# GpSimd instead of VectorE for the weight scales and for the inverse roots of queries and keys in a two-layer hybrid trunk

## The chip, the core and the metric

The kernel runs on one core of one Trainium2 chip. The metric is the device time of one execution in microseconds (us); the number that counts is the median of the runs.

## The reference

`x` is 512 tokens by 2048 columns. Two layers follow one another, each with one mixer of three parallel branches:

```python
h = rmsnorm(x, norm_g)                       # over 2048 columns
proj = h @ w_in                              # 2048 x 7696, float32
y_conv = B * (conv3(C * H) + bias) * silu(G)            # 4 x 512 columns
q, k = rmsnorm(sb_q, qn_g), rmsnorm(sb_k, kn_g)         # per head of 128
y_sb   = stick_breaking(q, k, sb_v) * silu(sb_g)        # 8 heads of 128
y_gla  = rmsnorm(gla(gl_q, gl_k, gl_v, decay(gl_lr))) * silu(gl_g)   # 4 heads
x = x + concat(y_conv, y_sb, y_gla) @ w_out  # 2048 x 2048
```

All weights are float32 in HBM and are read once per execution. What the change touches is not a step of the reference itself but two helpers: a power of two by which each block of weights is scaled before it is split into half-precision parts, and `rsqrt(mean(q*q) + eps)` of the query and key heads.

## The kernel before, in words

**Blocks of weights.** A layer's weights are cut into 38 blocks of 256 columns (one of 272): 30 of `w_in`, 8 of `w_out`; 76 in all, numbered along `specs`. A block is loaded by two DMAs of 1 MB (`fetch`, L341) into one of two staging tiles `st`. Then, for every block but the first:

1. `wmax` (L352): ScalarE squares both halves and adds them up per partition, two instructions of 128x2048, into `wm`.
2. `wscale`: GpSimd adds the sums up over the partitions (`partition_all_reduce`, L362, tile `wgm`). VectorE adds the two halves (L363, `wq`), masks the exponent (L371), and makes two powers of two by integer arithmetic on the bits: `ws` (L375), the scale, and `wp` (L377), from which `wu` (L379) follows, the factor that undoes the scale behind the matmul.
3. `whi` (L415): ScalarE writes `wh = half(st * ws)`. `wlo` (L421): VectorE writes `wl = half(st * ws - wh)`. One pair per half block; three tiles of each kind exist, so that the second half of a block waits until TensorE has read a half of the block before.
4. TensorE multiplies three times (high by high, high by low, low by high).

For 3 of the 8 blocks of `w_out` in layer 0 and 4 in layer 1 (`QUICK`) seven sums of sub-blocks take the place of eight products; ScalarE and VectorE split each of the seven (L450, L451) and VectorE makes the sums in place (L456 to L462). TensorE works them off at L698 with evictions at L709 to L727 between.

**Order.** `weights()` hands out block i, fetches block i + 2 and lets block i + 1 be scaled and split, at a raised priority; `issue_after` puts ScalarE's squares of a block behind the last `wh` of the block before it. Beyond that, and outside the first 40 us or so, which stand in an order written by hand for VectorE and ScalarE, a scheduler orders each engine's instructions when the program is built. Each engine works its own list off in order; an instruction that waits holds up those behind it.

**Stages of a layer**, with the times of layer 0 in the trace: GLA projections and the short convolution (to some 280 us), four rounds of stick-breaking attention (280 to 680), each of four blocks (V, gate, Q, K), the rest of the convolution (to 715), the eight blocks of `w_out` (to 870), whose last block is interleaved with the norm of the next layer.

**Query and key.** For each of the 16 Q and K blocks ScalarE copies the result out of PSUM (`raw`, L1198) and squares it (L1200), VectorE adds up over each head (`qs`, L1201) and makes eight inverse roots per partition: `qu` (L1203), `rsqrt_bits` (L207 to L214: a first guess from the bits, then three Newton steps of three instructions), a product with `wu` (L1206), all of 128x8. Then it scales `raw` (L1209 for Q, 64 instructions at L1214 for K), and ScalarE (L1218) and VectorE (L1219) split the result into `qp`, which is transposed by DMA.

Of the kernel before, what the change touches and what calls it, by code (L numbers as in the profile page):

```python
# [8 lines left out]
I32 = mybir.dt.int32  # L9
U8 = mybir.dt.uint8  # L10
AF = mybir.ActivationFunctionType
ALU = mybir.AluOpType
# [5 lines left out]
P = 128  # L18
EPS = 1e-6
# [20 lines left out]
def hybrid_trunk(ctx, tc, x, norm_g, w_in, conv_w, conv_b, sb_qn_g, sb_kn_g,  # L40
                 gla_w_up, gla_b_up, gla_on_g, w_out, out):
    nc = tc.nc
    V, S, G, T = nc.vector, nc.scalar, nc.gpsimd, nc.tensor
# [23 lines left out]
    def nm(s):  # L67
        uid[0] += 1
        return f"{s}_{uid[0]}"

    def sm(n, tag, bufs=None):
        return small.tile([P, n], F32, tag=tag, name=nm(tag), bufs=bufs)

    def wk(shape, tag, bufs=None, dt=F32):
        return work.tile(shape, dt, tag=tag, name=nm(tag), bufs=bufs)
# [4 lines left out]
    def bank(pool, tag):  # L80
        return pool.tile([P, 512], F32, tag=tag, name=nm("ps" + tag))
# [72 lines left out]
    r = 0  # L154
# [16 lines left out]
    def allmax(src, n, tag):  # L171

        gm = sm(n, tag + "gm")
        G.partition_all_reduce(gm, src, P, RED.absmax)
        return gm
# [28 lines left out]
    def rsqrt_bits(dst, src, scale, n, tag):  # L204

        m = sm(n, tag + "rm")
        V.tensor_scalar(m, src, scale, EPS, ALU.mult, ALU.add)  # L207
        r = sm(n, tag + "r0")
        V.tensor_scalar(r.bitcast(I32), m.bitcast(I32), -0.5, float(0x5F375A86), ALU.mult, ALU.add)
        t = sm(n, tag + "rt")  # L210
        for i in range(3):
            V.tensor_tensor(t, r, r, ALU.mult)
            V.scalar_tensor_tensor(t, t, -0.5, m, ALU.mult, ALU.mult)
            V.scalar_tensor_tensor(dst if i == 2 else r, t, 1.5, r, ALU.add, ALU.mult)  # L214

    identb = const.tile([P, P], BF16, tag="identb", name="identb")
    V.tensor_copy(identb, ident)
# [25 lines left out]
    xun = const.tile([P, depth], F32, tag="xun", name="xun")  # L243
# [73 lines left out]
    mixun = {}  # L317
# [37 lines left out]
    def wscale(i):  # L355

        l, src, cols = specs[i]

        m = sm(1, "wq")
        if i:  # L360
            gm = sm(2, "wgm")
            G.partition_all_reduce(gm, peak.pop(i), P, RED.add)  # L362
            V.tensor_scalar(m, gm[:, 0:1], gm[:, 1:2], 2.0 ** -120, ALU.add, ALU.max)  # L363
        else:

            ps = bank(psm, "m")[:, :1]
            pk = peak.pop(i)
            for j, (a, b) in enumerate(((ones, pk[:, 0:1]), (ones, pk[:, 1:2]), (pk[:, 2:3], pk[:, 2:3]))):
                T.matmul(ps, a.to_broadcast([P, P]), b, start=j == 0, stop=j == 2)
            V.tensor_scalar(m, ps, 2.0 ** -120, None, ALU.max)  # L370
        V.tensor_scalar(m.bitcast(I32), m.bitcast(I32), 0x7F000000, None, ALU.bitwise_and)  # L371

        lift = int(i in quick)
        sc = sm(1, "ws")
        V.tensor_scalar(sc.bitcast(I32), m.bitcast(I32), -0.5, float((204 - lift) << 23), ALU.mult, ALU.add)  # L375
        p2 = sm(1, "wp")
        V.tensor_scalar(p2.bitcast(I32), m.bitcast(I32), 0.5, float((50 + lift) << 23), ALU.mult, ALU.add)  # L377
        u = sm(1, "wu", bufs=6)
        V.tensor_tensor(u, p2, mixun[l] if src is w_out else xun[:, l:l + 1], ALU.mult)  # L379
        loaded[i] = ([], u)  # L380
        scales[i] = sc

# [179 lines left out]
    xhigh(0, 0, mix)  # L562
    xsquare(1)
    wscale(0)
    whi0(0, 0, S)
    whi0(0, 1, V)
# [40 lines left out]
    for l in range(depth):  # L607
# [3 lines left out]
        def project_cols():  # L611

            w, u = weights()
            ps = [bank(psp, "p") for _ in range(2)]
            for h in range(2):
                wh, wl = w[h]
                for c, o in enumerate(ps):
                    cs = slice(c * P, (c + 1) * P)
                    for kk in range(HK):
                        k = h * HK + kk  # L620
                        st_ = (h == 0 and kk == 0)
                        en = (h == 1 and kk == HK - 1)
                        T.matmul(o, wh[:, kk, cs], xh[:, :, k, :], start=st_, stop=False)  # L623
                        T.matmul(o, wh[:, kk, cs], xl[:, :, k, :], start=False, stop=False)  # L624
                        T.matmul(o, wl[:, kk, cs], xh[:, :, k, :], start=False, stop=en)  # L625
            return ps, u
# [153 lines left out]
        def mixscale(j, m, tag, top=11.0):  # L780

            pow2(pmix[:, j:j + 1], m, -top, tag)
            s_ = sm(1, tag + "smix")
            V.reciprocal(s_, pmix[:, j:j + 1])
            return s_
# [77 lines left out]
        for tag in ("qT", "kT"):  # L863
            ps, u = project_cols()
# [3 lines left out]
            gm = allmax(mx, 2, tag)  # L868
            m = sm(1, tag + "m")
            V.tensor_tensor(m, gm[:, 0:1], gm[:, 1:2], ALU.max)  # L870
            p2 = sm(1, tag + "p2")
# [15 lines left out]
        for p in range(2):  # L887
            ps, u = project_cols()
            gmx = sm(1, "ggm")
            gg.append(gate(ps, u, gmx))  # L890
            m = sm(1, "gb")
# [208 lines left out]
        def go():  # L1100
            if later:
                later.pop(0)()
# [64 lines left out]
        for j in range(4):  # L1167
            bm = sm(2, "bm")
            ps, u = project_toks(xh, xl)

            vhl = wk([P, 2, NT, GW], "v", dt=F16)
            vh, vl = vhl[:, 0], vhl[:, 1]
            for b in range(2):
                bs = slice(2 * b, 2 * b + 2)
                v3 = ps[b].rearrange("p (a c) -> p a c", a=2)
                S.activation(vh[:, bs, :], v3, AF.Copy, scale=2.0 ** -14)
                V.scalar_tensor_tensor(vl[:, bs, :], v3, 2.0 ** -14, vh[:, bs, :], ALU.mult, ALU.subtract)
            V.tensor_reduce(bm[:, 0:1], vh, AX.XY, ALU.max, apply_absolute_value=True)
            vu = sm(2, "vu")
            V.tensor_scalar(vu[:, 0:1], u, 2.0 ** 14, None, ALU.mult)  # L1180
            V.tensor_scalar(vu[:, 1:2], u, 1.0, None, ALU.mult)
            go()
            ps, u = project_cols()
            g = gate(ps, u, bm[:, 1:2], True)
            gm = allmax(bm[:, 0:1], 1, "b")
            m = sm(1, "sbm")
            V.scalar_tensor_tensor(m, gm, vu[:, 0:1], bm[:, 1:2], ALU.mult, ALU.mult)
            s_ = mixscale(2 + j, m, "b")
            go()
            qkT = []  # L1190
            for gain in (None, kg[:, l, :]):
                ps, u = project_toks(xh, xl)

                sq = sm(8, "qs")
                raw = wk([P, NT, GW], "raw", 1)
                for b in range(2):
                    rb = raw[:, 2 * b:2 * b + 2, :]
                    S.activation(rb, ps[b].rearrange("p (a c) -> p a c", a=2), AF.Copy)  # L1198
                    e = wk([P, 2 * GW], "e")
                    S.activation(e, rb.rearrange("p a c -> p (a c)"), AF.Square)  # L1200
                    V.tensor_reduce(sq[:, 4 * b:4 * b + 4], e.rearrange("p (a c) -> p a c", c=P), AX.X, ALU.add)  # L1201
                u2 = sm(1, "qu2")
                V.tensor_scalar(u2, u, u, 1.0 / P, ALU.mult, ALU.mult)  # L1203
                rs = sm(8, "qr")
                rsqrt_bits(rs, sq, u2, 8, "q")
                V.tensor_scalar(rs, rs, u, None, ALU.mult)  # L1206
                if gain is None:
                    r8 = raw.rearrange("p a (h c) -> p (a h) c", c=P)
                    V.tensor_tensor(r8, r8, rs.rearrange("p (a o) -> p a o", o=1).to_broadcast([P, 8, P]), ALU.mult)  # L1209
                else:  # L1210
                    for t in range(NT):
                        for hh in range(2):
                            rp = raw[:, t, hh * P:(hh + 1) * P]
                            V.scalar_tensor_tensor(rp, rp, rs[:, 2 * t + hh:2 * t + hh + 1], gain, ALU.mult, ALU.mult)  # L1214

                top = 2.0 ** 10 if gain is None else 1.0
                parts = wk([P, 2, NT * GW], "qp", 1, F16)
                S.activation(parts[:, 0], raw.rearrange("p t c -> p (t c)"), AF.Copy, scale=top)  # L1218
                V.scalar_tensor_tensor(parts[:, 1], raw.rearrange("p t c -> p (t c)"), top, parts[:, 0],  # L1219
                                       ALU.mult, ALU.subtract)  # L1220
                nT_ = wk([P, 2, NT, 2, P], "kT" if qkT else "qT", dt=F16)
                for i in range(2):
                    nc.sync.dma_start_transpose(nT_[:, i].rearrange("p t h c -> p (t h) c"), parts[:, i])
                qkT.append(nT_)
                go()
            attend(j, *qkT, vh, vl, vu, g, s_)
# [28 lines left out]
        for gi in range(NG):  # L1255
# [22 lines left out]
            else:  # L1278
                ps, u = project_toks(mh, ml, (11, 2, 3) if not gi else ())
# [31 lines left out]
```

## Time and profile before

| what | value |
|---|---|
| median of 3 runs | 1720.0 us (1718.39 to 1720.52) |
| profiled execution, own time | 1721.89 us |
| its span | 1720.1 us |
| granted TensorE clock | 0.997 |
| VectorE (DVE) busy | 1166.7 us (68%), 2149 instructions |
| ScalarE (ACT) busy | 1022.4 us (59%), 1243 instructions |
| GpSimd (POOL) busy | 63.5 us (4%), 104 instructions |
| DMA | 204.95 MB, mean 119 GB/s |

A group row of the profile reads: line, engine, operation, output<-inputs, shapes, xcount | busy us in total, mean ns of one | idle time of the engine just before them, and what ended it. A row of the waits reads: engine and line that waited <- who ended the wait: us in total, number of waits, longest. A timeline row reads: start in us, length in us, engine, line, operation, and in brackets the engine's idle time before it and what ended that.

### The profile page before, as it was taken

The numbers are of one execution on the slowest core, as the hardware profiler recorded it, in microseconds if no ns is written. First come the engines' busy times: TensorE is split into PE (matmuls) and PEld (weight loads), VectorE is DVE, ScalarE is ACT, GpSimd is POOL, SyncE is SP. The second block draws the span as 40 slices with busy tenths as digits, with TensorE's granted clock in tenths as the row PEclk, the third lists the DMA queues.
The fourth block names the chain that finished last, engine by engine and source line by source line (L and its number), as shares of the span: only waits on it lengthen the run. The fifth ranks groups of instructions, "written<-read, shape, count | busy, mean of one in ns | idle before, by whom it ended". The sixth has DMA issues, their size and how long they took to land. (4 is left out here: it accounts for less than half of the span.)

```text
span 1720.1 us, 32415 instructions
## 1 busy us (share of the span) xinstructions
PE 1702.0 (99%) x13770; PEld 1227.2 (71%) x13770; DVE 1166.7 (68%) x2149; ACT 1022.4 (59%) x1243; POOL 63.5 (4%) x104
## 2 busy tenths in 40 slices
PE   7999999999999999999999999999999999999998
PEld 5744557878787764799986454668686868548998
DVE  8566897566666656786675588974656566567883
ACT  7558676555555555566655575864555555545661
POOL 1100000000000000000010000000000000000000
PEclk9999999999999999999999999999999999999999
DMA  7323321344444445145544231223544433343441
GB/s 251 98 98 98 99 98 54 113 120 126 119 121 123 129 123 153 61 156 181 181 116 148 83 108 55 99 98 111 126 127 126 125 108 108 116 137 123 148 155 45
DMA packets 266641, 204.95 MB, mean 119 GB/s; under 512 B 93362, under 2 KB 265724, under 8 KB 265984
## 3 DMA queue, kind: packets, MB, share of 16 engines
q1 hardware_dynamic: 257488, 193.42, 37.1%
q10 hardware_dynamic: 9008, 9.45, 1.6%
q8 instruction: 108, 1.77, 0.4%
q14 instruction: 37, 0.30, 0.1%
HBM read 173.36 MB, written 8.39 MB: 106 GB/s over the span
## 5 line engine op out<-in xcount | busy, mean ns | idle before, releaser
L421 DVE SCALAR_TENSOR_TENSOR wl<-st,ws,wh 128x2048 f16<-128x2048 f32 (+1 forms) x138 | 324.4, 2352 | 205.3 <-ACT wh L415 205.3
L415 ACT ACTIVATE wh<-st,ws 128x2048 f16<-128x2048 f32 (+1 forms) x136 | 272.0, 2003 | 247.0 <-PE psp L633 111.0
L633 PE MATMUL psp<-wh,m 128*128 128x256 f16 x1216 | 331.5, 273 | 0.0
L632 PE MATMUL psp<-wl,m 128*128 128x256 f16 x1216 | 331.4, 273 | 0.0
L631 PE MATMUL psp<-wh,m 128*128 128x256 f16 x1216 | 331.4, 273 | 0.0
L352 ACT ACTIVATE junk<-st 128x2048 uint8<-128x2048 f32 (+1 forms) x150 | 285.5, 1903 | 4.9 <-DMA st<-in_w_out_dram 3.0
L633 PE MATMUL psp<-wh,x 128*128 128x256 f16 x768 | 209.3, 273 | 0.0
L632 PE MATMUL psp<-wl,x 128*128 128x256 f16 x768 | 209.3, 273 | 0.0
L631 PE MATMUL psp<-wh,x 128*128 128x256 f16 x768 | 209.3, 273 | 0.0
L623 PE MATMUL psp<-m,wh 128*128 128x512 f16 x512 | 194.0, 379 | 0.0
L624 PE MATMUL psp<-x,wh 128*128 128x512 f16 x512 | 194.0, 379 | 0.0
L624 PE MATMUL psp<-m,wh 128*128 128x512 f16 x512 | 194.0, 379 | 0.0
L623 PE MATMUL psp<-x,wh 128*128 128x512 f16 x512 | 194.0, 379 | 0.0
L625 PE MATMUL psp<-x,wl 128*128 128x512 f16 x512 | 193.9, 379 | 0.0
L625 PE MATMUL psp<-m,wl 128*128 128x512 f16 x512 | 193.9, 379 | 0.0
L625 PEld LDWEIGHTS <-wl 128*128 128x128 f16 x1024 | 100.2, 98 | 119.7
L624 PEld LDWEIGHTS <-wh 128*128 128x128 f16 x1024 | 100.2, 98 | 118.7 <-issue 2.6
L623 PEld LDWEIGHTS <-wh 128*128 128x128 f16 x1024 | 100.2, 98 | 117.5 <-issue 1.9
L631 PEld LDWEIGHTS <-m 128*128 128x128 f16 x1216 | 119.0, 98 | 13.9
L633 PEld LDWEIGHTS <-m 128*128 128x128 f16 x1216 | 119.0, 98 | 13.9
L632 PEld LDWEIGHTS <-m 128*128 128x128 f16 x1216 | 119.0, 98 | 13.8
L363 DVE TENSOR_SCALAR wq<-wgm 128x1 f32<-128x1 f32 x75 | 15.9, 212 | 111.1 <-POOL wgm L362 111.1
(356 smaller groups left out, 2665.0 us busy)
## 6 DMA issues: line engine op xcount, KB each, us to landing
st<-in_w_in_dram SPq DMA_DIRECT2D x120, 1024.0 KB, 7.7
st<-in_w_out_dram SPq DMA_DIRECT2D x32, 1024.0 KB, 7.6
x<-in_x_dram SPq DMA_DIRECT2D x4, 1024.0 KB, 5.1
qT<-in_x_dram ACTq DMA_DIRECT2D x8, 512.0 KB, 6.4
qT<-xs ACTq DMA_DIRECT2D x8, 512.0 KB, 3.9
xs<-x SPq DMA_DIRECT2D x14, 256.0 KB, 3.8
out_dram<-kT SPq DMA_DIRECT2D x14, 256.0 KB, 2.1
th<-za SPq DMA_TRANSPOSE x64, 3.1
```

The costliest lines, as they stand in the source:

```text
L352: S.activation(junk(HK * n).rearrange("p (k n) -> p k n", k=HK), staged[i][h][:, :, :n], AF.Square, accum_out=peak[i][:, h:h + 1])
L363: V.tensor_scalar(m, gm[:, 0:1], gm[:, 1:2], 2.0 ** -120, ALU.add, ALU.max)
L415: lasthi[i] = S.activation(wh[:, :, :n], staged[i][h][:, :, :n], AF.Copy, scale=scales[i])
L421: V.scalar_tensor_tensor(wl[:, :, :n], staged[i][h][:, :, :n], scales[i], wh[:, :, :n], ALU.mult, ALU.subtract)
L623: T.matmul(o, wh[:, kk, cs], xh[:, :, k, :], start=st_, stop=False)
L624: T.matmul(o, wh[:, kk, cs], xl[:, :, k, :], start=False, stop=False)
L625: T.matmul(o, wl[:, kk, cs], xh[:, :, k, :], start=False, stop=en)
L631: T.matmul(o, ah[:, t, k, :], wh[:, kk, :n], start=st_, stop=False, skip_group_check=True)
L632: T.matmul(o, ah[:, t, k, :], wl[:, kk, :n], start=False, stop=False, skip_group_check=True)
L633: T.matmul(o, al[:, t, k, :], wh[:, kk, :n], start=False, stop=en, skip_group_check=True)
```

## The change

`wscale` runs on GpSimd for every block but the first. GpSimd gets no mask of bits: the scale is a first guess of the inverse root from the bits, rounded to a power of two by a multiplication with 2^23 + 1 and two subtractions; the factor that undoes it is made from the scale by integer arithmetic. It takes seven instructions behind the all-reduce, of which the fifth gives `ws` and the seventh `wu`. `rsqrt_bits`, `qu` and the product with `wu` run on GpSimd too; a Newton step has four instructions there where VectorE had three, because the fused form of two tensors and a scalar is split.

```diff
     def rsqrt_bits(dst, src, scale, n, tag):
         m = sm(n, tag + "rm")
-        V.tensor_scalar(m, src, scale, EPS, ALU.mult, ALU.add)
+        G.tensor_scalar(m, src, scale, EPS, ALU.mult, ALU.add)
         r = sm(n, tag + "r0")
-        V.tensor_scalar(r.bitcast(I32), m.bitcast(I32), -0.5, float(0x5F375A86), ALU.mult, ALU.add)
+        G.tensor_scalar(r.bitcast(I32), m.bitcast(I32), -0.5, float(0x5F375A86), ALU.mult, ALU.add)
         t = sm(n, tag + "rt")
         for i in range(3):
-            V.tensor_tensor(t, r, r, ALU.mult)
-            V.scalar_tensor_tensor(t, t, -0.5, m, ALU.mult, ALU.mult)
-            V.scalar_tensor_tensor(dst if i == 2 else r, t, 1.5, r, ALU.add, ALU.mult)
+            G.tensor_tensor(t, r, r, ALU.mult)
+            G.tensor_tensor(t, t, m, ALU.mult)
+            G.tensor_scalar(t, t, -0.5, 1.5, ALU.mult, ALU.add)
+            G.tensor_tensor(dst if i == 2 else r, t, r, ALU.mult)
...
         m = sm(1, "wq")
+        E = G if i else V
         if i:
             gm = sm(2, "wgm")
             G.partition_all_reduce(gm, peak.pop(i), P, RED.add)
-            V.tensor_scalar(m, gm[:, 0:1], gm[:, 1:2], 2.0 ** -120, ALU.add, ALU.max)
+            E.tensor_scalar(m, gm[:, 0:1], gm[:, 1:2], 2.0 ** -120, ALU.add, ALU.max)
...
-        V.tensor_scalar(m.bitcast(I32), m.bitcast(I32), 0x7F000000, None, ALU.bitwise_and)
-
         lift = int(i in quick)
-        sc = sm(1, "ws")
-        V.tensor_scalar(sc.bitcast(I32), m.bitcast(I32), -0.5, float((204 - lift) << 23), ALU.mult, ALU.add)
-        p2 = sm(1, "wp")
-        V.tensor_scalar(p2.bitcast(I32), m.bitcast(I32), 0.5, float((50 + lift) << 23), ALU.mult, ALU.add)
-        u = sm(1, "wu", bufs=6)
-        V.tensor_tensor(u, p2, mixun[l] if src is w_out else xun[:, l:l + 1], ALU.mult)
+        sc, c, u = sm(1, "ws"), sm(1, "wp"), sm(1, "wu", bufs=6)
+        E.tensor_scalar(m.bitcast(I32), m.bitcast(I32), -0.5, float(0x5F3759DF + ((14 - lift) << 23)), ALU.mult, ALU.add)
+        E.tensor_scalar(c, m, 2.0 ** 23 + 1, None, ALU.mult)
+        E.tensor_tensor(m, c, m, ALU.subtract)
+        E.tensor_tensor(sc, c, m, ALU.subtract)
+        E.tensor_scalar(c.bitcast(I32), sc.bitcast(I32), -1.0, float(254 << 23), ALU.mult, ALU.add)
+        E.tensor_tensor(u, c, mixun[l] if src is w_out else xun[:, l:l + 1], ALU.mult)
...
                 u2 = sm(1, "qu2")
-                V.tensor_scalar(u2, u, u, 1.0 / P, ALU.mult, ALU.mult)
+                G.tensor_scalar(u2, u, u, 1.0 / P, ALU.mult, ALU.mult)
                 rs = sm(8, "qr")
                 rsqrt_bits(rs, sq, u2, 8, "q")
-                V.tensor_scalar(rs, rs, u, None, ALU.mult)
+                G.tensor_scalar(rs, rs, u, None, ALU.mult)
```

In the built programs this reads as follows. VectorE's compute instructions go from 2149 to 1568. GpSimd's list gains 781 instructions of arithmetic (525 of the weight scales, 256 of the inverse roots). It also gains instructions that the diff doesn't show: the all-reduce and the arithmetic belong to two different libraries of GpSimd's code, and wherever one follows the other the build inserts an instruction that loads the other library. There is 1 of them before and there are 158 after, two for nearly every block of weights. They stand in GpSimd's own list, in order: load, all-reduce, load, seven steps of arithmetic, and in Q and K blocks the sixteen of the inverse roots behind those. ScalarE's list keeps its order but for small moves: behind K and V blocks the last `wh` and the first square of the next block now stand ahead of `qp` (L1218) or of the last `za` (L1134), where they stood behind it.

## The prediction

> **What bounds the kernel now.** I read the engine totals first, then TensorE's waits, then the waits of the engines that feed it, and last the timelines around single blocks. The totals:
>
> ```profile
> PE 1702.0 (99%) x13770; PEld 1227.2 (71%) x13770; DVE 1166.7 (68%) x2149; ACT 1022.4 (59%) x1243; POOL 63.5 (4%) x104
> ```
>
> TensorE is busy for 1702.0 of 1720.1 us. Its waits (line that waited <- who ended it: us, times, longest) add up to some 14 us:
>
> ```profile
> PE psz L235 <- DVE identb L217: 3.7, 1, 3.7
> PE psp L738 <- DMA m<-raw: 2.8, 1, 2.8
> PE psp L738 <- ACT wh L405: 2.1, 1, 2.1
> PE psz L512 <- DVE x L521: 1.8, 1, 1.8
> PE psp L698 <- ACT g L709: 1.3, 1, 1.3
> ...
> PE psp L698 <- DVE g L711: 0.8, 1, 0.8
> ...
> PE psp L698 <- DVE wl L451: 0.2, 1, 0.2
> ```
>
> So little can be won: the first rows lie in the head of the kernel, before any scale of this change, and what relief for VectorE could touch is the L698 rows, 2.3 us, and the 2.8 us. What can be lost is larger: each microsecond by which a block's halves come late beyond the slack of their chain is one in which TensorE stands. The chain of a block is squares on ScalarE, all-reduce on GpSimd, scale, `wh`, `wl`, products. The change touches its middle.
>
> **The chain now.** The waits of the whole kernel on the scale's way:
>
> ```profile
> DVE wq L363 <- POOL wgm L362: 111.1, 61, 6.2
> ...
> ACT wh L415 <- DVE ws L375: 9.9, 7, 2.8
> ...
> ACT wh L415 <- DVE wp L377: 9.3, 8, 1.6
> ...
> ACT wh L450 <- DVE wp L377: 2.4, 2, 1.2
> ...
> ACT wh L450 <- DVE wu L379: 0.9, 1, 0.9
> ...
> ACT wh L450 <- DVE ws L375: 0.9, 1, 0.9
> ```
>
> VectorE stands 111.1 us behind the all-reduce, in order, and ScalarE waits on the scale itself in 19 places. The steps (start, us, engine, line; idle before in brackets):
>
> ```profile
> 322.87 0.21 DVE L363 TENSOR_SCALAR wq<-wgm 128x1 f32<-128x1 f32 x1 [2.14 <-POOL wgm L362]
> 323.12 0.15 DVE L371 TENSOR_SCALAR wq<-wq 128x1 int32<-128x1 int32 x1
> 323.31 0.15 DVE L375 TENSOR_SCALAR ws<-wq 128x1 int32<-128x1 int32 x1
> ```
>
> ```profile
> L362 POOL PARTITION_ALL_REDUCE wgm<-wm x75: 400/400/2256, 40.3 to 1676.0; - x75
> ```
>
> From 322.87 to the end of `ws` at 323.46 are 0.6 us; with the all-reduce's 0.40 and two handovers of some 0.1 each, the peak turns into a scale in about 1.2 us.
>
> **The new chain.** It is: handover 0.2, all-reduce 0.40, load of the arithmetic's library, five operations to `ws`. The load that fetches the all-reduce's library stands ahead of the all-reduce, so it can run while GpSimd waits for the squares; only the second is on the path. Neither a GpSimd operation of this kind nor such a load stands in the trace, so both are bounded.
>
> *An operation:* the nearest rows are the all-reduce above (0.40, the upper end) and the smallest memset:
>
> ```profile
> L1297 POOL MEMSET const-float32-1.0<- 128x1 f32 x1 | 0.1, 100 | 0.0
> ```
>
> I take 0.25, the middle; five make 1.25 (0.5 to 2.0).
>
> *A load R:* the program before has one, between these two rows, and it shows no record of its own:
>
> ```profile
> 25.72 3.52 POOL L776 MEMSET m<- 128x4096 f16 x1 [23.11 <-DMA st<-in_w_in_dram]
> 30.31 0.76 POOL L174 PARTITION_ALL_REDUCE kgm<-kg  x2 [1.07 <-DVE xrt L201]
> ```
>
> The idle time is 1.07 us and an operand ended it, so that load took between 0 and 1.07. That library may have been left in place by the execution before, though, and a load that really brings code must move it. Transfers have these lengths here (issue to landing):
>
> ```profile
> st<-in_w_in_dram SPq DMA_DIRECT2D x120, 1024.0 KB, 7.7
> ...
> th<-za SPq DMA_TRANSPOSE x64, 3.1
> ```
>
> Ends: 0 and 7.7 us. I take 5.4, the middle between the two transfer rows: the one load that was seen need not have moved anything, and the new ones alternate, so each must. Latency from peak to scale is then 0.2 + 0.4 + 5.4 + 1.25 = 7.25 us, **6.0 more** than now. The Trainium skill, page "GPSIMD Engine Reference", section "Instruction dispatch", says that the first call to a freshly loaded kernel additionally pays about 6 us (5.95 measured) for the code; no run here shows it yet, and with 5.95 in place of 5.4 my sum below would be some 20 us higher, an estimate.
>
> *The inverse roots:* on VectorE they go from 419.49 to 422.56 (one foreign 0.75 in between), some 2.5 us net, for `rm`, `r0`, nine steps and the last product; `qu` is made earlier.
>
> ```profile
> 419.49 0.23 DVE L207 TENSOR_SCALAR qrm<-qs,qu 128x8 f32<-128x8 f32 x1
> ...
> 422.33 0.23 DVE L1206 TENSOR_SCALAR qr<-qr,wu 128x8 f32<-128x8 f32 x1
> 422.59 1.23 DVE L1209 TENSOR_TENSOR raw<-raw,qr 128x1024 f32<-128x1024 f32 x1
> ```
>
> On GpSimd they are fifteen dependent operations, 3.75 us (1.5 to 6.0): **1.25 more** in each of 16 Q and K blocks. They follow the scale's arithmetic without a load between. Behind them the next block's load and all-reduce are queued, but those wait for squares that come later anyway.
>
> **Term A, attention (300 to 660).** Here ScalarE has room, because its `wh` waits for TensorE to free a buffer:
>
> ```profile
> ACT wh L415 <- PE psp L633: 52.0, 19, 7.4
> ...
> ACT qp L1218 <- DVE raw L1214: 22.2, 4, 6.6
> ACT wh L415 <- PE psp L624: 19.9, 9, 3.9
> ```
>
> That is 71.9 us in 16 blocks, against which stand the later scales. One block as an example:
>
> ```profile
> 409.04 0.58 ACT L1198 ACTIVATE raw<-psp 128x512 f32<-128x512 f32 x1
> ...
> 429.73 1.91 ACT L352 ACTIVATE junk<-st 128x2048 uint8<-128x2048 f32 x1
> 431.55 0.19 ACT L352 ACTIVATION_READ_ACCUMULATOR junk<-st 128x1 f32 x1
> ...
> 436.29 2.00 ACT L415 ACTIVATE wh<-st,ws 128x2048 f16<-128x2048 f32 x1 [3.41 <-PE psp L633]
> ```
>
> The squares end at 431.74 and the next `wh` starts at 436.29: 4.55 us of room, 2.7 less than 7.25. Over the stage the chain gains 16 x 6.0 + 8 x 1.25 = 106 us per layer. In the four K blocks one `wh` and one square (2.00 + 1.91, some 4.0) now run while `qp` waits (22.2 us in that row), which gives back 16. So 90 against 71.9: ScalarE falls 18 us behind in a layer. TensorE feels only a part. ScalarE's evictions free its banks early:
>
> ```profile
> 420.37 0.27 PE L631 MATMUL psp<-wh,x 128*128 128x256 f16 x1
> ```
>
> The bank evicted at 409.62 is used again at 420.37, 10.75 us later; a lag up to that costs nothing. 18 - 10.75 is about 7.4 us, in two layers **15 us** (0 if R is under 4, 88 at 7.7).
>
> **Term B, layer 0's `w_out` (735 to 880).** There the scale already ends ScalarE's waits:
>
> ```profile
> ACT wh L450 <- DVE wp L377: 2.4, 2, 1.2
> ACT wh L415 <- DVE ws L375: 1.7, 2, 1.1
> ...
> ACT wh L450 <- DVE ws L375: 0.9, 1, 0.9
> ...
> ACT wh L415 <- DVE wp L377: 0.3, 1, 0.3
> ```
>
> Six waits x 6.0 are 36 us. TensorE's own waits here are small, so some slack behind `wh` exists, which I can't read off; half reaches TensorE: **18** (0 to 36).
>
> **Term C, the rest.** 13 of the 19 waits on the scale lie elsewhere, in stages with much VectorE work between: 1 us each, **13** (0 to 78, were nothing hidden). **Term D**, the last blocks: L698's waits grow with a later `wh`, less the relief of VectorE: **+2** (-5 to +10).
>
> The DMAs are not moved in their queues; a staging tile comes free behind `wl`, later by the lag alone, and a load lands in 7.7 us of a block's 22 (360 / 16), so that is hidden while the lag is under 14. VectorE loses 581 instructions; that costs nothing and wins nothing beyond 2.8 + 2.3 us, for TensorE waits for nothing else from it.
>
> Sum: 15 + 18 + 13 + 2 = 48; 1721.9 + 48 = 1770 against the profiled execution (span 1720.1 and 1.8 around it), which lies 1.9 over the median: **1768 us**.
>
> **The rivals.**
>
> *The load is cheap (R at most 1.07).* For it: the only load in the trace. Against it: that one may have moved nothing. The chain gains 0.2 + 0.4 + 1.07 + 1.25 - 1.2 = 1.7 us; A is 16 x 1.7 + 10 - 16 = 21 against 71.9, so 0; B 6 x 1.7 / 2 = 5; D -2 to 0: about 1723 (1718 to 1728).
>
> *Faster.* VectorE no longer stands 111.1 us behind the all-reduce, nor does it make the roots, and what it hands out comes sooner. The place is L698's waits (2.3) and the DMA row (2.8): at most 5.1 us, 1715 to 1717. It decides if the load and five operations together take no more than about 0.8 us, what VectorE's 0.6 and a handover take now. Beside VectorE's wide instructions GpSimd is also stretched:
>
> ```profile
> 1598.34 2.26 POOL L362 PARTITION_ALL_REDUCE wgm<-wm  x1 [14.50 <-ACT junk L352]
> ```
>
> which is against it.
>
> *Both loads on the path.* If a library is brought in only when its first instruction is reached, the one ahead of the all-reduce isn't hidden either, and R counts twice: 11.4 us more instead of 6.0. A: 16 x 11.4 + 10 - 16 - 71.9 - 10.75 = 94, in two layers 188; B 34; C 13 x 6.4 / 2 = 42; D 8: 272, so 1992. For it: nothing in the trace shows when code is brought. Against it: GpSimd idles 20 us and more ahead of most all-reduces. The Trainium skill's section named above puts the price on the first call, not on the load, so this rival is its reading; no run here shows it.
>
> *The change doesn't do what it says* is excluded by the built program: VectorE's instructions are gone and GpSimd's are there.
>
> **How the numbers follow.** Forecast (R of 3 to 7.7, one on the path; 1725 to 1855): 0.56, as a load must move code. At 7.7: A 88, B 25, C 18, D 4, 135 in all, so 1855. Cheap load: 0.24. Faster: 0.08. Both loads: 0.12. The range leaves the last out and reaches into the faster case: 1716 to 1855. 0.2%, about what can be told from no change here, is 3.4 us (1716.6 to 1723.4): half of the cheap case falls into it, 0.12, the other half and the rest are slower: 0.80; faster 0.08.
>
> **What would show it.** Right: between the all-reduce and the first step on GpSimd a gap of some 5 us in every block; steps of 0.2 to 0.3 us; ScalarE's waits for `ws` from GpSimd some 7 us long in 735 to 880, and its waits for L633 and L624 in attention all but gone; new TensorE waits on `psp`, most of all in 735 to 880. VectorE's 111.1 us are gone. Wrong: a gap of 1 us or less (cheap), a second gap ahead of the all-reduce after the squares (both loads), operations over 0.4 us, or TensorE waiting where neither A, B nor C lies.

## The result

The changed kernel takes **2241.4 us** (median of 4 runs, 2239.09 to 2245.02) against 1720.3 us (1718.39 to 1721.29): a ratio of 1.303, 95% interval 1.301 to 1.306. It is slower by 521 us, where 48 were forecast, and the range ended at 1855.

### The profile page after: what moved, and what is told of

Same layout as the page of the kernel before. It is cut to its first block, busy times and chain, and to the rows that moved or that the text cites. A ratio compares the mean times of both kernels' runs of the same rounds, so it can differ in the third digit from the quotient of the medians.

```text
span 2239.3 us, 32871 instructions
## 1 busy us (share of the span) xinstructions
PE 1826.5 (82%) x13770; PEld 1277.7 (57%) x13770; DVE 1086.6 (49%) x1568; ACT 1017.5 (45%) x1243; POOL 239.5 (11%) x885
## 4 chain that ended last, share of the span: by engine, by line
issue 45%; ACT 22%; DVE 15%; PE 9%; POOL 9%; POOLq 0%; ACTq 0%; DVEq 0%
ACT junk L353 9%; ACT wh L416 8%; PE psp L739 3%; DVE wl L422 3%; POOL wgm L364 2%; DVE za L1130 2%; POOL wq L365 1%; DVE wl L452 1%; PE psp L699 1%; PE psp L624 1%; PE psp L625 1%; POOL wp L376 1%; PE psp L626 1%; DVE zw L1132 1%; ACT za L1135 1%
## 5 line engine op out<-in xcount | busy, mean ns | idle before, releaser
L422 DVE SCALAR_TENSOR_TENSOR wl<-st,ws,wh 128x2048 f16<-128x2048 f32 (+1 forms) x138 | 324.5, 2354 | 686.1 <-ACT wh L416 685.9
L416 ACT ACTIVATE wh<-st,ws 128x2048 f16<-128x2048 f32 (+1 forms) x136 | 271.5, 1999 | 757.9 <-POOL ws L378 733.0
L632 PE MATMUL psp<-wh,m 128*128 128x256 f16 x1216 | 343.0, 282 | 57.8 <-ACT raw L1199 27.4
L633 PE MATMUL psp<-wl,m 128*128 128x256 f16 x1216 | 342.7, 282 | 10.3 <-DVE wl L422 10.3
L634 PE MATMUL psp<-wh,m 128*128 128x256 f16 x1216 | 342.4, 282 | 0.0
L624 PE MATMUL psp<-x,wh 128*128 128x512 f16 x512 | 202.7, 396 | 55.6 <-ACT kT L878 19.6
L624 PE MATMUL psp<-m,wh 128*128 128x512 f16 x512 | 201.1, 393 | 53.8 <-ACT kT L878 18.6
L625 PEld LDWEIGHTS <-wh 128*128 128x128 f16 x1024 | 103.2, 101 | 238.7 <-issue 130.7
L632 PE MATMUL psp<-wh,x 128*128 128x256 f16 x768 | 214.6, 279 | 24.9 <-ACT raw L1199 24.9
L634 PE MATMUL psp<-wh,x 128*128 128x256 f16 x768 | 214.8, 280 | 0.0
L626 PE MATMUL psp<-x,wl 128*128 128x512 f16 x512 | 201.8, 394 | 0.0
L625 PE MATMUL psp<-x,wh 128*128 128x512 f16 x512 | 201.8, 394 | 0.0
L625 PE MATMUL psp<-m,wh 128*128 128x512 f16 x512 | 201.0, 393 | 0.0
L626 PE MATMUL psp<-m,wl 128*128 128x512 f16 x512 | 200.5, 392 | 0.0
L624 PEld LDWEIGHTS <-wh 128*128 128x128 f16 x1024 | 103.0, 101 | 137.0 <-issue 27.7
L633 PEld LDWEIGHTS <-m 128*128 128x128 f16 x1216 | 122.7, 101 | 68.4 <-issue 50.8
L634 PEld LDWEIGHTS <-m 128*128 128x128 f16 x1216 | 122.9, 101 | 30.5 <-issue 12.1
L364 POOL PARTITION_ALL_REDUCE wgm<-wm x75 | 40.3, 537 | 925.9 <-ACT junk L353 851.3
L632 PEld LDWEIGHTS <-m 128*128 128x128 f16 x1216 | 122.9, 101 | 27.8 <-ACT m L1042 9.6
```

Of the source, the lines that this page charges most:

```text
L416: lasthi[i] = S.activation(wh[:, :, :n], staged[i][h][:, :, :n], AF.Copy, scale=scales[i])
L422: V.scalar_tensor_tensor(wl[:, :, :n], staged[i][h][:, :, :n], scales[i], wh[:, :, :n], ALU.mult, ALU.subtract)
L632: T.matmul(o, ah[:, t, k, :], wh[:, kk, :n], start=st_, stop=False, skip_group_check=True)
L633: T.matmul(o, ah[:, t, k, :], wl[:, kk, :n], start=False, stop=False, skip_group_check=True)
L634: T.matmul(o, al[:, t, k, :], wh[:, kk, :n], start=False, stop=en, skip_group_check=True)
```

## The profile after

The page of the changed kernel: busy times, granted clock of TensorE in 40 slices, and the chain that ended last.

```profile
PE 1826.5 (82%) x13770; PEld 1277.7 (57%) x13770; DVE 1086.6 (49%) x1568; ACT 1017.5 (45%) x1243; POOL 239.5 (11%) x885
...
PEclk9888899989898998998888888999998989899999
...
issue 45%; ACT 22%; DVE 15%; PE 9%; POOL 9%; POOLq 0%; ACTq 0%; DVEq 0%
```

The same row of the kernel before, whose chain the profile follows over 48% of the span only:

```profile
PE 45%; DMA 2%; DVE 1%; ACT 0%; issue 0%; SPq 0%; DVEq 0%; ACTq 0%
```

TensorE's work is the same 13770 matmuls, but the chain now hardly touches it: 9% of a chain that covers the whole span, where nearly all of the chain was TensorE's. Of the 519 us that the span grew, 124 are longer busy times of TensorE (1826.5 against 1702.0) and 395 are TensorE standing. GpSimd is busy for 11% and is not short of time either. What is long is a share of which no engine is the owner: "issue" is time in which an engine waited for nothing that the profile shows. The waits of the whole kernel say whose:

```profile
ACT wh L416 <- POOL ws L378: 733.0, 68, 25.7
POOL wq L365 <- issue: 713.2, 75, 11.4
DVE wl L422 <- ACT wh L416: 685.9, 98, 17.3
...
ACT wh L451 <- POOL ws L378: 45.2, 7, 10.0
```

75 times GpSimd stands ahead of the first step of the scale, 713.2 / 75 = 9.5 us each, at the place where the built program loads the library of the arithmetic. ScalarE waits 733.0 + 45.2 us for the scale, 75 times, VectorE 685.9 us for ScalarE, and the row of ScalarE's waits for TensorE in attention (71.9 us per layer before) is gone. GpSimd in two blocks:

```profile
405.30 0.41 POOL L364 PARTITION_ALL_REDUCE wgm<-wm  x1 [10.12 <-ACT junk L353]
415.00 0.32 POOL L365 TENSOR_SCALAR wq<-wgm 128x1 f32<-128x1 f32 x1 [9.29 <-issue]
415.40 0.19 POOL L375 TENSOR_SCALAR wq<-wq 128x1 int32<-128x1 int32 x1
415.67 0.23 POOL L376 TENSOR_SCALAR wp<-wq 128x1 f32<-128x1 f32 x1
415.99 0.19 POOL L377 TENSOR_TENSOR wq<-wp,wq 128x1 f32<-128x1 f32 x1
416.26 0.19 POOL L378 TENSOR_TENSOR ws<-wp,wq 128x1 f32<-128x1 f32 x1
...
425.63 1.24 POOL L364 PARTITION_ALL_REDUCE wgm<-wm  x1 [8.26 <-ACT junk L353]
436.84 0.31 POOL L365 TENSOR_SCALAR wq<-wgm 128x1 f32<-128x1 f32 x1 [9.97 <-issue]
```

The all-reduce starts as soon as ScalarE's square releases it: the load ahead of it is hidden. The one behind it is not: 9.29 and 9.97 us. The five steps to `ws` take 1.45 us, 0.3 apart. From the last square to the scale it is 0.1 + 0.5 + 9.5 + 1.45, about 11.6 us, 10.4 more than before.

What this does on ScalarE, in one block of attention:

```profile
540.80 0.58 ACT L1199 ACTIVATE raw<-psp 128x512 f32<-128x512 f32 x1
...
541.41 0.63 ACT L1201 ACTIVATE e<-raw 128x512 f32<-128x512 f32 x1
553.12 2.00 ACT L416 ACTIVATE wh<-st,ws 128x2048 f16<-128x2048 f32 x1 [11.08 <-POOL ws L378]
555.02 0.58 ACT L1199 ACTIVATE raw<-psp 128x512 f32<-128x512 f32 x1
555.63 0.63 ACT L1201 ACTIVATE e<-raw 128x512 f32<-128x512 f32 x1
...
565.02 1.06 ACT L1219 ACTIVATE qp<-raw 128x1024 f16<-128x1024 f32 x1 [5.97 <-DVE raw L1210]
565.98 1.99 ACT L416 ACTIVATE wh<-st,ws 128x2048 f16<-128x2048 f32 x1
```

ScalarE stands 11.08 us in front of `wh`, and **behind** `wh` in its list stand the second eviction (`raw` at 555.02), its square, and everything that VectorE and GpSimd make of them (`qp` waits another 5.97 us), and then the second `wh`, behind which come the next squares. So squares, load, `wh`, evictions, roots, `wh` and the next squares form one loop without a gap, 29 us a block in attention (463.7 / 16, in the table below) where TensorE needed 22 (357.1 / 16). TensorE's longest waits are therefore not for the weights but for what stood behind them in the list:

```profile
PE psp L632 <- ACT raw L1199: 52.4, 10, 7.0
PE psz L1117 <- DMA kT<-qp: 50.3, 8, 7.6
PE psz L914 <- ACT m L908: 39.9, 6, 10.9
PE psp L624 <- ACT kT L878: 38.2, 2, 19.6
```

The longest single wait for a scale, the 25.7 us above, has three loads in it. In one block of GLA in each layer an all-reduce of GLA (`kTgm`) stands in GpSimd's list between the second and the third step of a scale, with a load before and behind it:

```profile
175.41 0.37 POOL L174 PARTITION_ALL_REDUCE kTgm<-kTmx  x1 [6.54 <-issue]
182.81 0.26 POOL L376 TENSOR_SCALAR wp<-wq 128x1 f32<-128x1 f32 x1 [7.03 <-issue]
```

The eviction `kT` (L878), for which TensorE waits 19.6 us, stands behind the `wh` of this scale.

Where the time came from, stage by stage (from the end of the instruction that writes `ws` of one block to that of a later one; microseconds):

| stage (blocks) | before | after | more | the prediction's term |
|---|---|---|---|---|
| to the scale of block 1 | 41.3 | 58.1 | 17 | none |
| GLA, convolution, layer 0 (1 to 13) | 260.7 | 358.4 | 98 | C |
| attention, layer 0 (13 to 29) | 357.1 | 463.7 | 107 | A: 7.4 |
| `w_out`, layer 0 (29 to 39) | 224.2 | 304.2 | 80 | B: 18 |
| GLA, convolution, layer 1 (39 to 51) | 267.3 | 358.7 | 91 | C, with the above: 13 |
| attention, layer 1 (51 to 67) | 357.0 | 463.6 | 107 | A: 7.4 |
| `w_out`, layer 1 (67 to 75) | 173.5 | 197.9 | 24 | D: 2 |

With the tail (-4) this is the 519 us of the spans. Every stage lost, and those that the forecast took for covered lost most.

## Theories and experiments

**Theory 1**: the latency from square to scale carries the loss, whatever it is made of. **Theory 2**: the loads disturb (fetching code beside the weights, GpSimd beside VectorE). **Theory 3**: the inverse roots. **Theory 4**, formed after the first runs: the latency, *in lists that were ordered for a short one*. Each ratio is to the kernel before on the same chip, with its 95% interval.

**Latency without loads.** To the kernel before, `n` fillings of an unused tile are added on GpSimd, and VectorE's first step waits for them (the last, small one supplies its constant):

```diff
-            G.partition_all_reduce(gm, peak.pop(i), P, RED.add)
-            V.tensor_scalar(m, gm[:, 0:1], gm[:, 1:2], 2.0 ** -120, ALU.add, ALU.max)
+            ar = G.partition_all_reduce(gm, peak.pop(i), P, RED.add)
+            least = sm(1, "least")
+            for n in range(10 + 1):
+                with tc.issue_after(ar.ins):
+                    ar = G.memset(pause, 0) if n < 10 else G.memset(least, 2.0 ** -120)
+            V.tensor_scalar(m, gm[:, 0:1], gm[:, 1:2], least, ALU.add, ALU.max)
```

Three:

> The kernel before, with three fillings of an unused tile (128x1024 bytes) on GpSimd between the all-reduce and VectorE's first step of the scale, which waits for them: some 3 us more from the last square to the scale in each of 75 blocks, and no library loaded. Theory 1 (the chain): the time follows this latency alone, whatever it is made of; the first 3 to 4 us of it vanish in ScalarE's waits for TensorE, so 1720 to 1765. Theory 2 (the loads disturb: fetching code, or GpSimd's arithmetic, slows other work): 1720 to 1730, as nothing is loaded.

Six:

> As the run with three fillings, with six: some 6 us more of latency. Theory 1: (6 - 3.5) x 75, so 1830 to 1930. Theory 2: 1740 to 1790, what the prediction's own sum gives for 6 us of latency (48 us).

Ten:

> As the run with three fillings, with ten: some 10 us more of latency, as the changed kernel has, with no load and no arithmetic on GpSimd. Theory 1: (10 - 3.5) x 75 = 490, so 2150 to 2250, the changed kernel but for its inverse roots. Theory 2: at most 1950, what the prediction's sum gives for that latency; the rest of the 521 us would then be the loads' disturbance.

Measured: 1734.2 (1.008, 1.006 to 1.010), 1752.7 (1.019, 1.017 to 1.021) and **1804.0** us (1.049, 1.047 to 1.051). Ten fillings do last as long as the load:

```profile
425.65 0.40 POOL L363 PARTITION_ALL_REDUCE wgm<-wm  x1 [12.27 <-ACT junk L353]
425.92 10.11 POOL L367 MEMSET pause<- 128x1024 uint8 x10
435.96 0.10 POOL L367 MEMSET least<- 128x1 f32 x1
```

yet they cost 83 us, not 490. Theory 1 as stated falls: with six and with ten fillings the time lies far below its ranges, and the same latency costs a sixth of what the changed kernel lost. Theory 2's ranges for these two hold, but they say only that something else carries the rest. ScalarE in the run with ten shows why:

```profile
425.46 0.58 ACT L1203 ACTIVATE raw<-psp 128x512 f32<-128x512 f32 x1
426.07 0.63 ACT L1205 ACTIVATE e<-raw 128x512 f32<-128x512 f32 x1
430.10 0.60 ACT L1203 ACTIVATE raw<-psp 128x512 f32<-128x512 f32 x1 [3.40 <-PE psp L638]
430.73 0.63 ACT L1205 ACTIVATE e<-raw 128x512 f32<-128x512 f32 x1
432.90 0.72 ACT L798 ACTIVATE m<-e,bsmix 128x512 f16<-128x512 f32 x1 [1.54 <-DVE e L1165]
437.99 1.06 ACT L1223 ACTIVATE qp<-raw 128x1024 f16<-128x1024 f32 x1 [4.37 <-DVE raw L1214]
438.96 1.99 ACT L420 ACTIVATE wh<-st,ws 128x2048 f16<-128x2048 f32 x1
442.23 2.00 ACT L420 ACTIVATE wh<-st,ws 128x2048 f16<-128x2048 f32 x1 [1.28 <-PE psp L638]
```

Here both evictions, their squares, `m` and `qp` stand *ahead* of both `wh`; they fill the ten microseconds, and in this block `wh` waits for no scale. The order is the scheduler's, made with the fillings in the program. The loads of the changed kernel appear only in the built program: its lists are those of a scale that is there at once.

**Loads without latency**: one GpSimd operation behind each all-reduce, whose result nobody reads.

```diff
             V.tensor_scalar(m, gm[:, 0:1], gm[:, 1:2], 2.0 ** -120, ALU.add, ALU.max)
+            G.tensor_scalar(sm(1, "idle"), gm[:, 0:1], gm[:, 1:2], 2.0 ** -120, ALU.add, ALU.max)
```

> The kernel before, with one more GpSimd operation behind each all-reduce (it adds the two sums, and nobody reads the result). The libraries are loaded as often as in the changed kernel, but no scale waits for them. Theory 1: 1718 to 1740; only where two all-reduces follow each other within 16 us can the second come late. Theory 2: 1800 to 2100.

Measured: 1797.1 (1.045, 1.043 to 1.046), above Theory 1's range and just under Theory 2's. The trace shows the mechanism of the chain, at another place. A pair of loads takes some 15 us:

```profile
404.54 0.41 POOL L362 PARTITION_ALL_REDUCE wgm<-wm  x1 [11.15 <-ACT junk L352]
414.53 0.31 POOL L364 TENSOR_SCALAR idle<-wgm 128x1 f32<-128x1 f32 x1 [9.58 <-issue]
420.60 0.50 POOL L174 PARTITION_ALL_REDUCE bgm<-bm  x1 [5.76 <-issue]
```

and where the next all-reduce is wanted earlier, it is late. GpSimd's groups of this run have that time as "issue" in the idle time ahead of the all-reduces:

```profile
L362 POOL PARTITION_ALL_REDUCE wgm<-wm x75 | 32.4, 432 | 818.7 <-ACT junk L352 751.1 <-issue 61.4 <-ACT e L451 6.3
...
L174 POOL PARTITION_ALL_REDUCE bgm<-bm x8 | 4.9, 607 | 47.4 <-issue 29.4 <-DVE za L1027 11.8 <-DVE za L1136 6.2
```

The loss stands at the start (9 us), in the GLA and convolution stages (31 and 22) and in layer 0's `w_out` (14). In the sixteen blocks of attention, with a load at every block as elsewhere, not a microsecond was lost (357 us per layer, as before): loading by itself disturbs nothing there.

**Arithmetic without the all-reduce**, from the changed kernel; each partition makes a scale of its own sums, so the sum over the partitions is left out (the constant of the first guess, not shown, makes up for its size).

```diff
-            gm = sm(2, "wgm")
-            G.partition_all_reduce(gm, peak.pop(i), P, RED.add)
+            gm = peak.pop(i)
```

> The changed kernel without the all-reduce of the weight scales: each partition makes its scale from its own two sums (times 128 in the constant), so the scale is left without its sum over the partitions. With that, nearly all loads go; the arithmetic stays on GpSimd. Theory 1 (the chain): five operations of 0.28 us are a latency like that of before, so 1712 to 1735. Theory 2 (GpSimd's arithmetic or its loads disturb): 1740 or more.

Measured: 1755.3 (1.021, 1.019 to 1.022): of the 521 us, 486 are gone with the loads. The time lies in the range given to Theory 2, but the other 35 us stand where loads remain, around the all-reduces at the start (9 us) and of GLA (L174; 11 and 15 us). TensorE's longest waits come from there:

```profile
PE psp L623 <- ACT kT L877: 21.7, 2, 11.0
```

**The two halves of the change.** The roots back on VectorE (the three groups of `G.` in `rsqrt_bits`, `qu` and the product are `V.` again); and the reverse, the kernel before with these alone on GpSimd.

> The changed kernel with the inverse roots back on VectorE, so only the weight scales are on GpSimd. Theory 1: fifteen operations of 0.28 us become 2.5 us in 16 blocks, 16 x 2 = 32 us less: 2195 to 2220. Theory 3 (the roots carry much of the loss, as they stand in ScalarE's way to the next block): under 2050.

> The kernel before with only the inverse roots on GpSimd. In the list of GpSimd the roots of a block now stand behind the next block's all-reduce and a load, so two pairs of loads for a Q or K block, none of them ahead of a scale. Theory 1: the queries and keys come some 10 us later in 16 blocks, of which 4 us vanish: 16 x 6 = 96, so 1780 to 1860. Theory 3: above 1950.

Measured: 2238.7 (1.302, 1.299 to 1.304) and 1720.1 (0.9999, 0.9989 to 1.0010). The weight scales carry all of it; Theory 3 falls. Theory 1's figures were missed too: it gave the roots 20 to 45 us in the one run and 60 to 140 in the other. The roots alone cost nothing although a load stands in front of them: in that kernel the load runs while GpSimd waits for VectorE's sums anyway,

```profile
POOL qrm L207 <- DVE qs L1202: 98.1, 10, 10.4
```

and the scale is VectorE's there, so no `wh` waits for a load of the arithmetic.

**An earlier start**, from the changed kernel (`firsthi` holds the first `wh` of a block, as `lasthi` the last):

```diff
-        with tc.issue_after(lasthi[i - 1].ins):
+        with tc.issue_after(firsthi.get(i - 1, lasthi[i - 1]).ins):
```

> The changed kernel with the squares of a block behind the first `wh` of the block before it, not behind its last, so that its load runs beside that block's second half. Same loads, same arithmetic. Theory 1: the second `wh` (2 us) and what ScalarE does between the halves (3 to 6 us) come out of the chain, 5 to 8 us in most blocks: 1750 to 1900. Theory 2: above 2150, as the loads are as many.

Measured: 2005.1 (1.165, 1.163 to 1.168), between the two. ScalarE's wait for the scale fell, but a new one came:

```profile
DVE raw L1211 <- POOL qr L1208: 107.8, 8, 18.0
ACT wh L416 <- POOL ws L378: 107.0, 12, 17.3
DVE raw L1216 <- POOL qr L1208: 98.5, 8, 13.2
```

733.0 us became 107.0, but the all-reduce of the next block now comes before the roots of this one in GpSimd's list, with its loads, and VectorE waits 206 us for `qr`.

**The order, tested by itself** (Theory 4). The run with ten fillings, with each engine's list held to that of the kernel before by added order-only edges (`inorder`, a table of places in the traced program for TensorE, VectorE and ScalarE):

```diff
+    def inorder(engine, order):
+        mine = [i for i in nc.cur_bb.bb.instructions if i.engine == engine]
+        for a, b in zip(order, order[1:]):
+            tc.add_manual_dep(mine[b], mine[a].name, mybir.DependencyInfo(
+                mybir.DependencyClass.NoSync, mybir.DependencyReason.DATA), reason="inorder")
```

> The run with ten fillings, with the lists of TensorE, VectorE and ScalarE held to those of the kernel before, instruction for instruction; only GpSimd's list is its own. Nothing is loaded. Theory 4 (the order): 10 us of latency cost 83 us where the scheduler knew of them and moved ScalarE's other work ahead of the waiting `wh`, and cost what the changed kernel lost where the lists were made for a latency of 1 us: 2150 to 2250 here. Theory 2 (the loads disturb): the order is not the cause, 1800 to 1850.

Measured: **2287.9** (1.330, 1.328 to 1.333), 38 us above Theory 4's range. No load, no moved arithmetic, and the whole loss is there, and some more: VectorE, which holds the first step in this kernel, stands behind the fillings in its own list, which in the changed kernel it doesn't, and ScalarE waits for it:

```profile
DVE wq L368 <- POOL least L367: 839.7, 75, 16.2
ACT wh L420 <- DVE wp L382: 420.1, 43, 12.4
ACT wh L420 <- DVE ws L380: 133.0, 12, 12.3
```

Then the reverse, the changed kernel with ScalarE's list held to that of the ten fillings:

> The changed kernel, with ScalarE's list held to that of the run with ten fillings (evictions and products for attention ahead of both `wh` of a block); all loads and all arithmetic on GpSimd stay as they are. Theory 4: 1800 to 1880, the 83 us of the ten fillings and something for the roots and for lists of the other engines that fit less well. Theory 2: above 2100.

Measured: 1921.5 (1.117, 1.115 to 1.119): 320 of the 521 us come back with the same instructions and loads, in another order: ScalarE's list is held, and the scheduler laid the lists of the other engines anew around it. The forecast of 1800 to 1880 was missed: 201 us are left. In attention, where the ten fillings cost nothing, it is some 28 us per layer. There the roots now stand in GpSimd's list behind the load of the scale, and `qp` waits longer for them than in the changed kernel (43.5 and 28.5 us there; GpSimd's own wait for the sums is down from 82.4 us to 1.9); ScalarE's wait for the scale is down from 733.0 us:

```profile
ACT wh L416 <- POOL ws L378: 148.0, 42, 8.0
ACT qp L1219 <- DVE raw L1210: 89.8, 8, 12.9
ACT qp L1219 <- DVE raw L1215: 77.4, 8, 16.6
```

The other 146 us stand outside attention (17 at the start, 28 to 38 in each other stage, 7 won back in the tail); what makes them is not tested.

One operation moved, with as many loads, from the kernel before:

```diff
-            V.tensor_scalar(m, gm[:, 0:1], gm[:, 1:2], 2.0 ** -120, ALU.add, ALU.max)
+            G.tensor_scalar(m, gm[:, 0:1], gm[:, 1:2], 2.0 ** -120, ALU.add, ALU.max)
```

> The kernel before with one operation of the scale, the sum of the two halves, on GpSimd instead of VectorE; everything else stays on VectorE. As many loads as in the run in which nobody waits for them (1797), and ScalarE's list as in the kernel before but for some 20 places; but now each scale waits for a load. Theory 4: 2150 to 2230, nearly all of the loss with one moved instruction per block. Theory 2: under 1850, as the loads are the same.

Measured: 2256.2 (1.312, 1.309 to 1.314), 26 us above Theory 4's range, against 1797.1 with the same operation unread. One instruction of 0.3 us on another engine costs 536 us.

And ScalarE's list alone held, with ten fillings:

> As the run with ten fillings and the old lists, but only ScalarE's list is held to that of the kernel before; those of TensorE and VectorE are the scheduler's, made with the fillings known. Theory 4a (ScalarE's list alone carries the loss): 2150 to 2290, near the 2288 with three lists held. Theory 4b (it is VectorE's list, whose scale stands in front of its other work, or TensorE's): under 2000.

Measured: 2139.7 (1.244, 1.242 to 1.246), just under the range of 4a: with ScalarE's old list alone, 336 of the 484 us between 1804.0 and 2287.9 are there. It is no clean split, as the scheduler laid the lists of VectorE and TensorE anew around the held one.

**The prediction's own latency.** Six and three fillings with the three old lists:

> The run with six fillings, with the lists of TensorE, VectorE and ScalarE held to those of the kernel before: 6 us more of latency, just what the prediction assumed (6.0), with the lists that it assumed. If the prediction's sum was sound and only its price of a load too low: 1750 to 1790. If the sum itself failed (each block loses what exceeds a slack of some 2.5 us, 75 times): 1900 to 2020.

> The same with three fillings, 3 us more of latency. Sum sound: 1720 to 1735. A slack of some 2.5 us per block: 1735 to 1800. No slack at all, 75 x 3: 1940.

Measured: **1973.7** (1.149, 1.147 to 1.151) and 1772.1 (1.031, 1.030 to 1.033), beside 1718.2 on the same chip. So in the old lists 3.0 us cost 54, 6.1 us cost 256, 10.1 us (the run above) 568. From 3.0 to 6.1 each microsecond costs 65, from 6.1 to 10.1 it costs 78: the slope is near that of 75 blocks, each paying in full, above some 2.3 to 2.7 us that are free (each loss divided by 75, taken from the latency). The stages of the run with six, above the kernel before, are 9 (start), 44, 34, 51, 46, 34 and 32.

No variant beat the kernel before; the best, with the roots alone on GpSimd, is its equal. Theory 4 is what the runs show: a latency of 10 us without a load makes the whole loss in the old lists and a sixth of it in lists made for it, and an operation behind a load costs 459 us more when the scale waits for it than when nobody reads it.

## Why the prediction was wrong

**The bounds now**: right. Nothing was to be won: the roots' relief for VectorE gave 0.9999 of the time. **One load hidden, one on the path**: right, but for the few scales with an all-reduce of GLA between their steps; the rival with both fell, as the all-reduce starts right behind the square. **Steps of 0.25 us**: right, 0.3 apart. **Direction**: right. These carried the 0.80 for slower.

**The price of a load** (5.4, upper end 7.7): failed. It is 9.5 us on average, beyond the bound. The bound was a transfer of 1 MB that has nothing to do with a library. The size goes with the traffic, in three loads of the changed kernel (stretch, its length, then the busy times of PE, PEld, DVE, ACT, POOL, TensorE's clock, the DMAs' share and GB/s):

```profile
918.50:925.60 7.10, 5.21 (x30) 3.90 (x31) 3.94 (x11) 6.41 (x7) 0.00 (x0) 0.57 0.00 0
511.30:522.10 10.80, 10.80 (x101) 9.69 (x100) 1.42 (x3) 0.06 (x1) 0.01 (x2) 1.00 0.67 205
1306.00:1312.90 6.90, 0.00 (x0) 0.00 (x0) 1.27 (x8) 0.00 (x0) 0.02 (x1) 0.50 0.00 0
```

6.9 to 7.1 us with still queues, 10.8 beside the weights at 205 GB/s. In the run with the earlier start, 73 of these loads take 7.3 us on average (531.0 us), most of them with queues nearly still. That the traffic is the cause is read from such rows, not tested. The Trainium skill ("GPSIMD Engine Reference", "Instruction dispatch") has 5.95 us for this; the load ahead of an all-reduce agrees where the queues are still (5.76 above), the one ahead of the arithmetic doesn't.

**The sum from latency to time** failed too, and more. With the 10.4 us of the changed kernel it would give, by the working of its last rival, A 155, B 31, C 13 x 5.4 / 2 = 35, D 8: 229, where 519 were measured. So, by the prediction's own sum, the price of the load accounts for 181 of the 471 us that the forecast missed; the other 290 are the sum itself. With 6.1 us, just over the 6.0 that it assumed, and the old lists, it gave 48 and the chip 256. (In that run VectorE stands 543.2 us behind the fillings, which it would not on the prediction's path; but at ten fillings, where both can be compared, the loss is 568 against the changed kernel's 521, so this is the smaller part.) By terms:

- **C** (13 us for "the rest") is the worst: at 6 us the GLA and convolution stages lost 90, in the changed kernel 189. It counted only the waits on the scale that were there already, 13 of them, and put 1 us on each. But a wait that was absent before appears as soon as the scale is later than ScalarE. ScalarE waited for the scale 75 times after, 19 before. And it had no price for the loads around GLA's own all-reduces: with the loads alone, where no scale waits for the arithmetic, these stages lost 53.
- **A** (15): 68 at 6 us, 213 in the changed kernel. It pooled the 71.9 us of a layer's waits as if one block's slack could serve another, and then took off 10.75 us of early eviction. But the eviction is behind `wh` in the list: it is late with it, and its 10.75 us is no cushion for a lag that arises ahead of it in each block anew.
- **B** (18): 51 at 6 us, 80 in the changed kernel; the half taken off as slack behind `wh` wasn't there.
- **The roots** (1.25 us in 16 blocks, inside A): 0 by the runs, though their steps took 0.28 us, not 0.25.
- **D** (2, at most 10): 32 at 6 us, 24 in the changed kernel; and the start, which had no term, 9 and 17.

What the prediction never weighed is **the order**. It asked by how much a `wh` comes late; it had to ask what stands behind it. Each block's other work on ScalarE stands behind the waiting instruction, so the latency isn't laid beside that work but added to it. With the order for a long latency the same 10 us cost 83.

**TensorE's clock** was missing from the working as well. Where TensorE stands, its clock falls; the last row above has 0.50 with no matmul, and the mean went from 0.997 to 0.904. The same matmuls are busy for 124 us more. How much of that is in the time is not tested, for matmuls that take longer while TensorE would stand anyway cost nothing. The run with ten fillings and old lists has 0.895 without a load, so the clock follows the waits. The Trainium skill ("TensorE: Matmul & The Clock Gate", "Part 1: The HAM clock gate") says that half speed comes after an idle window of about 3.4 us; the row agrees in the half.

## What to carry to other kernels

Ask of a longer latency first what is queued behind the instruction that waits, on an engine that works in order: slack of others doesn't help what stands behind it, and 10 us of latency cost 83 or 568 us here by the order alone. Look in the built program for instructions that the source doesn't have; where the lists are laid for a short wait, such a load makes it a long one, and one moved operation of 0.3 us cost three tenths of this kernel's time. An operation that shares no library with its neighbours on GpSimd is moved together with the neighbour, or not at all.

## What the runs showed of the hardware

- Where GpSimd alternates between two libraries, a load that nothing hides takes 5.6 to 10.0 us ahead of an all-reduce (run with the loads alone) and 6.9 to 11.4 us ahead of arithmetic (changed kernel). A load runs while GpSimd waits for operands (of 925.9 us ahead of the 75 all-reduces in the changed kernel 15.4 are uncovered load). The profile's table of queues doesn't show its traffic: 41 packets in queue 14 with 158 loads, 37 before, 43 in the run with ten fillings and no such loads.
- Fillings of a tile need no load: 750 of them beside 75 all-reduces, 0.96 us each for 128x1024 bytes, and no idle time of kind "issue" ahead of either.
- Dependent GpSimd operations on 128x1 or 128x8 follow each other every 0.28 us or so, VectorE's every 0.20 us (inverse roots in the run with the roots alone on GpSimd, and before).
